# The scan state's decay product on VectorE, the high part of rotated q and k on GpSimd for two heads, and the RWKV output ordered behind a scan step

## The chip, the cores and the metric

The kernel runs on one core of one Trainium2 chip. The metric is the device time of one execution in microseconds (us). Before the change three runs gave 1136.71, 1142.31 and 1142.92 us, a median of 1142.31 us. The five engines have the profile's names here: PE is TensorE, DVE is VectorE, ACT is ScalarE, POOL is GpSimd, SP issues most DMAs.

## The reference, cut to what matters

Two layers of a diffusion backbone run over 512 latent tokens and 256 context tokens, 1024 channels, batch 1, all in float32. In each layer one input projection feeds three groups of mixers, and an output projection joins them. The two mixers that the change touches:

```python
def step(S, inp):                       # RWKV, per direction, 4 heads of 64x64 state
    w_t, k_t, v_t, a_t, b_t = inp[-5:]
    sa = jnp.einsum('bhvk,bhk->bhv', S, a_t)
    S = S * w_t[:, :, None, :] + sa[..., None] * b_t[:, :, None, :] + v_t[..., None] * k_t[:, :, None, :]
    y_t = jnp.einsum('bhvk,bhk->bhv', S, inp[0]) if with_output else None
    return S, y_t
# readout: y = y_fwd + y_bwd, normalised per head, times ln_g, plus ln_b and a bonus times v, times silu(z)

# attention: q and k are rotated by position, then two softmaxes per head are subtracted
q_l = apply_axial_rope(qk_heads(q_l), rope)
k_l = apply_axial_rope(qk_heads(k_l), rope)
p = jax.nn.softmax(s, axis=-1)
attn = p[:, :, 0] - lam * p[:, :, 1]
```

The kernel does not run the recurrence token by token. It works in chunks of 64 tokens: inside a chunk everything is matrix products, and only the state is carried from chunk to chunk.

## The kernel before, in words

**Input projection as filler.** Every float32 weight tile (`wraw`) is split into a high part `whi` (a cast on ACT, L265) and a low part `wlo` (a subtract on POOL or DVE, L268), and each product is three matmuls. These matmuls (tiles pcl, pcc, ptl, ptc, by a helper at L137) are handed out in small amounts by `fill(us)` between the steps of the RWKV scan, so PE has work while the other engines carry the state.

**The scan** (`rwkv_scan`, L841). There are 12 chunks in each direction, taken as 3 batches `b` of 4 steps `p`, both directions side by side: 24 steps in two layers. Ahead of a batch stand a first stage (the products `s`, masked on DVE into `R`, with the diagonal blocks `Dg`) and an inverse of small triangular blocks (tiles `Acc`, `invt`, on DVE). One step is this chain, each part waiting for the one before it:

1. PE: `ch<-zu,R`, 16 small matmuls of the state tile `zu` (values and state, one tile per direction).
2. DVE: two copies `gs<-ch` out of PSUM.
3. PE: `yps<-zu,rt` (ordered behind the second gs copy) and `ch<-gs,XT`.
4. ACT and DVE in turn: four copies `zu<-ch` (ACT at L968, DVE in the same loop).
5. PE: `ch<-zu,R` again.
6. DVE: four adds `zu<-pz,ch` make the state for the next step, where `pz` is the old state times the chunk's decay `pc`.

The product `pz` (L947) is four multiplies of 64x128 elements per step on POOL, 88 in all, since the last step of each layer needs none. It needs only the state at the start of the step; its reader is part 6. The step's output is copied from `yps` on ACT (L991) or added on DVE. The tile framework's scheduler turns the program into one fixed order per engine; an engine takes its instructions strictly in that order.

**Rotated q and k** (`attn_proj`, function `qk`, from L1110). Four heads, q and k, two layers: 16 times. ACT copies the projection into `qkr` (L1118), SP moves the partner halves into `qks` by DMA, then POOL multiplies by sin (L1124) and cos (L1125) and adds (L1126); for heads 2 and 3 (`QV`) cos and add are on DVE. ACT casts the sum into its high part (L1127, over `qks`), POOL (DVE for heads 2 and 3) subtracts for the low part (L1128), and two DMAs (L1129, L1130) store both. This runs inside the filler, so it falls among the scan steps.

**RWKV output** (`rwkv_out`, L1000). For each part of the tokens: values `Vs` are loaded, multiplied by the bonus (L1019) and raised by ln_b (L1021) on POOL; DVE takes the mean `mu`, a variance and a Newton inverse root on tiny tiles (`rs_y`, `rs_t`), and scales `Y`. In layer 0 the part for the context tokens is ready after batch 0; the scheduler may place it anywhere behind that.

Of the kernel before, what the change touches and what calls it, by code (L numbers as in the profile page):

```python
# [26 lines left out]
HD = 64  # L27
# [38 lines left out]
QV = (2,3)  # L66
# [40 lines left out]
def build(tc, A):  # L107
    nc = tc.nc
    ctx = ExitStack()
    S, G = nc.scalar, nc.gpsimd  # L110
# [17 lines left out]
    V = Vec()  # L128
# [63 lines left out]
    def small(n, tag, pool=None, bufs=2):  # L192
        return (pool or sm).tile([P, n], F32, tag=tag, bufs=bufs, name=tag)
# [641 lines left out]
    def rwkv_scan(l, st, rw, lat, cx):  # L835
# [5 lines left out]
        zu = {}  # L841
# [32 lines left out]
        for b in range(3):  # L874
# [44 lines left out]
            for p in range(4):  # L919
# [19 lines left out]
                for d in range(2):  # L939
                    gs[d] = rw.tile([P, 2, HD], F32, tag="gs", bufs=2, name="gs")  # L940
                    cp = V.tensor_copy(gs[d], pv[d][:, 0])
                if not end:
                    for d in range(2):
                        pz[d] = rw.tile([P, 2, HD], F32, tag="pz", bufs=2, name="pz")
                        for h in range(2):
                            hr = slice(h * 64, h * 64 + 64)
                            G.tensor_tensor(out=pz[d][hr], in0=zu[d][hr, :, h, :],  # L947
                                            in1=prepd[d][1][hr, :, cc[d][1]].unsqueeze(2).to_broadcast([64, 2, HD]),
                                            op=ALU.mult)
                fill(F["a"] if want_y else F["n"])  # L950
# [45 lines left out]
                zu = nz  # L996
        lin["on"] = lin["dve"] = False

    def rwkv_out(l, st, yr, rw):
        n = NL if l == L - 1 else NT  # L1000
        zr = rw.tile([P, 2, NT], F32, tag="kkn", name="zr")
        nc.sync.dma_start(out=zr[:, :, :n], in_=zrd[l].rearrange("a p t -> p a t")[:, :, :n])
        Y = st["Y"]
        lng = rw.tile([P, 2, 2, HD], F32, tag="lng", name="lng")
        for h in range(2):
            nc.scalar.dma_start(out=lng[h * 64:h * 64 + 64].rearrange("p a b v -> p (a b v)"),
                                in_=A["lngb"][l, h:h + 1, :].to_broadcast([64, 256]))
        for c0, nch in ((0, 8),) if l == L - 1 else ((8, 4), (0, 8)):
            nu = nch * 2
            Yu = Y[:, c0:c0 + nch].rearrange("p c a v -> p (c a) v")  # L1010
            bon = st["bon"][:, 2 * c0:2 * c0 + nu]
            Vs = rw.tile([P, 8, 2, HD], F32, tag="wk", bufs=WK, name="Vs")
            for h in range(2):
                for hp in range(2):
                    o = hp * P + h * 64
                    nc.sync.dma_start(out=Vs[h * 64:h * 64 + 64, 0:nch, hp, :],
                                      in_=vd[l][c0 * 64:(c0 + nch) * 64, o:o + 64].rearrange("(c t) v -> t c v", t=64))
            Vu = Vs[:, :nch].rearrange("p c a v -> p (c a) v")
            G.tensor_tensor(out=Vu, in0=Vu, in1=bon.unsqueeze(2).to_broadcast([P, nu, HD]), op=ALU.mult)  # L1019
            for hp in range(2):  # L1020
                G.tensor_tensor(out=Vs[:, :nch, hp], in0=Vs[:, :nch, hp],  # L1021
                                in1=lng[:, 1, hp].unsqueeze(1).to_broadcast([P, nch, HD]), op=ALU.add)
            mu = small(24, "mu")
            V.tensor_reduce(out=mu[:, :nu], in_=Yu, axis=AX.X, op=ALU.add)
            V.tensor_scalar_mul(mu[:, :nu], mu[:, :nu], -1.0 / HD)
            V.tensor_tensor(out=Yu, in0=Yu, in1=mu[:, :nu].unsqueeze(2).to_broadcast([P, nu, HD]), op=ALU.add)
            sq = rw.tile([P, 24, HD], F32, tag="wk", bufs=WK, name="gnsq")
            S.activation(sq[:, :nu], Yu, AF.Square)
            var = small(24, "var")
            V.tensor_reduce(out=var[:, :nu], in_=sq[:, :nu], axis=AX.X, op=ALU.add)  # L1030
            V.tensor_scalar(out=var[:, :nu], in0=var[:, :nu], scalar1=1.0 / HD, scalar2=GN_EPS,
                            op0=ALU.mult, op1=ALU.add)
            rs = small(24, "gnrs")
            rsqrt(var[:, :nu], nu, rs[:, :nu])
            V.tensor_tensor(out=Yu, in0=Yu, in1=rs[:, :nu].unsqueeze(2).to_broadcast([P, nu, HD]), op=ALU.mult)
            for hp in range(2):
                yh = Y[:, c0:c0 + nch, hp]
                V.tensor_tensor(out=yh, in0=yh, in1=lng[:, 0, hp].unsqueeze(1).to_broadcast([P, nch, HD]), op=ALU.mult)
                V.tensor_tensor(out=yh, in0=yh, in1=Vs[:, :nch, hp], op=ALU.add)
                fill(F["o"] if hp == 0 else F["o2"])  # L1040
                lin["next"] = MG & 64
                pb = psalt("yT")
                for c in range(nch):
                    for h in range(2):
# [60 lines left out]
    def attn_proj(l, lat, cx):  # L1105
# [8 lines left out]
        def qk(h, fk=()):  # L1114
            for i in range(2):
                t, sw = fst("qkr"), fst("qks")
                yield from proj_ch(l, lat, cx if i else cxx,
                                   lambda o, c, nn: S.mul(t[:, c:c + nn], o, 1.0 if i else 0.125), fk=fk)  # L1118
                nn = NT if i else n
                for j in range(2):  # L1120
                    for x in range(2):
                        a, b = j * 64 + x * 32, j * 64 + 32 - x * 32
                        pin((S if SW else nc.sync).dma_start(out=sw[a:a + 32, :NL], in_=t[b:b + 32, :NL]), 2)
                G.tensor_tensor(out=sw[:, :NL], in0=sw[:, :NL], in1=sinT, op=ALU.mult)  # L1124
                (V if h in QV else G).tensor_tensor(out=t[:, :NL], in0=t[:, :NL], in1=cosT, op=ALU.mult)  # L1125
# [607 lines left out]
```

## Time and profile before

| | |
|---|---|
| runs | 1136.71, 1142.31, 1142.92 us, median 1142.31 |
| the profiled execution | 1136.55 us, of which its span (first to last instruction) is 1134.8 us |
| busy, PE / DVE / ACT / POOL | 1029.8 / 714.8 / 523.7 / 446.5 us |
| share of the span | 91% / 63% / 46% / 39% |
| chain that ended last | PE 41%, DVE 15%, ACT 7%, POOL 6%, issue 6% |
| POOL, wlo (L268) and pz (L947) | 181.6 and 39.5 us busy |

Busy is time in which an engine executes. PE is at 91%, so what can be won lies in its idle stretches and in stretches with a lowered clock; the chain shows that the other engines set the end for about a third of the span. An engine's idle time is put down to what released it ("idle before <-releaser"). L118 is the helper through which all DVE operations go, L137 and L135 the helpers for matmuls, so tiles tell operations apart. Times in the trace count from the start of the span.

### The profile page before, as it was taken

How to read it: one execution, taken by the hardware profiler on the slowest of the kernel's cores; microseconds unless marked ns; L12 is line 12 of the kernel's file. 1: busy time of each engine (PE TensorE's matmuls, PEld its weight loads, DVE VectorE, ACT ScalarE, POOL GpSimd, SP SyncE). 2: the span in 40 equal slices, each digit the busy share in tenths (PEclk: the TensorE clock that was granted, in tenths of full speed). 3: DMA queues.
4: the chain of work that ended last, by engine and by line, in shares of the span. 5: the costliest groups of instructions: out<-in, count | busy, mean ns of one | idle time of the engine just before them, and what ended most of it. 6: DMA issues, size and time to landing. Idle time of an engine off the chain costs nothing.

```text
span 1134.8 us, 25347 instructions
## 1 busy us (share of the span) xinstructions
PE 1029.8 (91%) x9850; PEld 844.0 (74%) x9850; DVE 714.8 (63%) x1736; ACT 523.7 (46%) x1330; POOL 446.5 (39%) x452
## 2 busy tenths in 40 slices
PE   4899989999699998989899899998988999888897
PEld 1577968777588867878787786876767897777775
DVE  3530558788467262489847857776985824579944
ACT  3432553453363223478724564654353532248731
POOL 0311534434736522432222345255475454431322
PEclk9999999999999999989999999999998999999999
DMA  9574322212334466654052452232223345546143
GB/s 354 178 242 134 86 79 57 58 35 71 133 85 130 131 192 194 201 172 103 15 190 85 139 180 86 70 96 71 78 79 103 99 127 160 165 149 183 48 158 111
DMA packets 92088, 142.55 MB, mean 126 GB/s; under 512 B 28192, under 2 KB 36416, under 8 KB 91968
## 3 DMA queue, kind: packets, MB, share of 16 engines
q1 hardware_dynamic: 88512, 136.14, 39.0%
q10 hardware_dynamic: 3456, 4.80, 1.3%
q8 instruction: 77, 1.26, 0.5%
q14 instruction: 43, 0.35, 0.1%
HBM read 110.99 MB, written 25.71 MB: 120 GB/s over the span
## 4 chain that ended last, share of the span: by engine, by line
PE 41%; DVE 15%; ACT 7%; issue 6%; POOL 6%; DMA 3%; SPq 1%; ACTq 0%; DVEq 0%; POOLq 0%
PE pcl L137 14%; PE op L137 6%; PE ptl L137 3%; PE pcc L137 3%; PE av L137 2%; PE ptc L137 2%; PE sc L137 2%; DVE mx L118 2%; PE ch L135 1%; DMA mraw<-in_mod_w_dram 1%; ACT e L1250 1%; DVE bk L118 1%; DVE rs_t L118 1%; PE yps L135 1%; POOL wlo L268 1%
## 5 line engine op out<-in xcount | busy, mean ns | idle before, releaser
L268 POOL TENSOR_TENSOR wlo<-wraw,whi 128x512 fp32r<-128x512 f32 x134 | 181.6, 1358 | 303.1 <-ACT whi L265 261.6
L137 PE MATMUL pcl<-lat,whi 128*128 128x512 f32 (+1 forms) x928 | 294.6, 394 | 2.6 <-issue 1.6
L137 PEld LDWEIGHTS pcl<-lat,whi 128*128 128x128 f32 x928 | 169.8, 190 | 40.0 <-issue 7.5
L137 PE MATMUL pcl<-lat,wlo 128*128 128x512 f32 (+1 forms) x464 | 184.6, 398 | 2.9 <-POOL wlo L268 2.9
L265 ACT CAST whi<-wraw 128x512 fp32r<-128x512 f32 x144 | 88.8, 619 | 149.6 <-DMA wraw<-in_w_in_dram 38.7
L137 PE MATMUL pcc<-ctx,whi 128*128 128x256 f32 x576 | 111.4, 290 | 2.2 <-DVE ctx L118 1.7
L137 PEld LDWEIGHTS pcl<-lat,wlo 128*128 128x128 f32 x464 | 87.8, 189 | 27.1 <-issue 4.5
L137 PEld LDWEIGHTS pcc<-ctx,whi 128*128 128x128 f32 x576 | 94.0, 195 | 9.2 <-issue 3.2
L137 PE MATMUL pcc<-ctx,wlo 128*128 128x256 f32 x288 | 83.7, 291 | 2.0 <-DVE wlo L118 2.0
L137 PE MATMUL ptl<-whi,lat 128*128 128x256 f32 x384 | 79.2, 293 | 0.0
L1250 ACT ACTIVATE e<-sc,mx 128x768 f32<-128x768 f32 (+1 forms) x80 | 66.3, 831 | 15.9 <-DVE mx L118 10.4
L118 DVE TENSOR_REDUCE mx<-sc 128x1 f32<-128x768 f32 (+1 forms) x72 | 63.9, 921 | 14.7 <-PE sc L137 14.7
L137 PE MATMUL av<-vA,aT 128*128 128x128 f32 x416 | 58.7, 285 | 10.1 <-ACT aT L1285 10.0
L137 PEld LDWEIGHTS av<-vA,aT 128*128 128x128 f32 x416 | 54.2, 194 | 16.0 <-ACT aT L1285 12.9
L137 PEld LDWEIGHTS ptl<-whi,lat 128*128 128x128 f32 x384 | 63.1, 195 | 2.0 <-issue 0.5
L118 DVE TENSOR_TENSOR R<-s,cs 128x384 f32<-128x384 f32 (+1 forms) x96 | 47.0, 530 | 19.6 <-PE s L135 18.9
L137 PEld LDWEIGHTS pcc<-ctx,wlo 128*128 128x128 f32 x288 | 55.9, 194 | 4.6 <-DVE wlo L118 2.2
L137 PE MATMUL sc<-KH,QS 128*128 128x256 f32 (+1 forms) x144 | 52.8, 380 | 4.5 <-ACT e L1250 2.9
L947 POOL TENSOR_TENSOR pz<-zu,pc 64x128 f32<-64x128 f32 x88 | 39.5, 449 | 43.2 <-DVE zu L118 38.5
L137 PE MATMUL ptl<-wlo,lat 128*128 128x256 f32 x192 | 56.1, 292 | 0.0
L137 PE MATMUL sc<-KL,QS 128*128 128x256 f32 (+1 forms) x144 | 46.3, 342 | 0.0
L118 DVE COPY zu<-ch 64x128 f32<-64x128 f32 x48 | 14.1, 294 | 47.8 <-ACT zu L968 41.8
(448 smaller groups left out, 2403.6 us busy)
## 6 DMA issues: line engine op xcount, KB each, us to landing
wraw<-in_w_in_dram SPq DMA_DIRECT2D x144, 256.0 KB, 2.7
mraw<-in_mod_w_dram SPq DMA_DIRECT2D x96, 256.0 KB, 4.5
KH<-qd SPq DMA_DIRECT2D x32, 192.0 KB, 3.8
oraw<-in_w_out_dram SPq DMA_DIRECT2D x20, 256.0 KB, 3.6
qd<-qks SPq DMA_DIRECT2D x12, 384.0 KB, 2.3
qd<-qkr SPq DMA_DIRECT2D x12, 384.0 KB, 2.5
qks<-qkr SPq DMA_DIRECT2D x64, 64.0 KB, 2.1
zu<-vd SPq DMA_DIRECT2D x96, 32.0 KB, 2.2
```

The costliest lines, as they stand in the source:

```text
L118: i = f(*a, **k)
L135: tc.keep_in_program_order(nc.tensor.matmul(*a, **k))
L137: i = nc.tensor.matmul(*a, **k)
L265: S.copy(hi, raw)
L268: eng.tensor_tensor(out=lo, in0=raw, in1=hi.bitcast(F32), op=ALU.subtract)
L947: G.tensor_tensor(out=pz[d][hr], in0=zu[d][hr, :, h, :], in1=prepd[d][1][hr, :, cc[d][1]].unsqueeze(2).to_broadcast([64, 2, HD]), op=ALU.mult)
L1250: ac(S.activation(ej[:, c], pb[:, c], AF.Exp, bias=mx[:, i:i + 1], accum_out=den[:, u["h"] * 6 + tt, j:j + 1]))
```

## The change

Three edits. The product `pz` is issued on DVE in place of POOL, 88 operations of 64x128 elements. The cast to the high part of rotated q and k is issued on POOL in place of ACT for heads 0 and 1, 8 of 16 casts (6 of 128x768 elements, 2 of 128x512). In the RWKV output, the bonus multiply on POOL and the mean on DVE are ordered behind the second `gs` copy of batch 2's first step; this is an order for the scheduler, not a semaphore.

```diff
--- before.py
+++ after.py
@@ -939,12 +939,14 @@
                 for d in range(2):
                     gs[d] = rw.tile([P, 2, HD], F32, tag="gs", bufs=2, name="gs")
                     cp = V.tensor_copy(gs[d], pv[d][:, 0])
+                if b == 2 and p == 0:
+                    st["step"] = cp.ins.name
                 if not end:
                     for d in range(2):
                         pz[d] = rw.tile([P, 2, HD], F32, tag="pz", bufs=2, name="pz")
                         for h in range(2):
                             hr = slice(h * 64, h * 64 + 64)
-                            G.tensor_tensor(out=pz[d][hr], in0=zu[d][hr, :, h, :],
+                            V.tensor_tensor(out=pz[d][hr], in0=zu[d][hr, :, h, :],
                                             in1=prepd[d][1][hr, :, cc[d][1]].unsqueeze(2).to_broadcast([64, 2, HD]),
                                             op=ALU.mult)
                 fill(F["a"] if want_y else F["n"])
@@ -1001,6 +1003,11 @@
         zr = rw.tile([P, 2, NT], F32, tag="kkn", name="zr")
         nc.sync.dma_start(out=zr[:, :, :n], in_=zrd[l].rearrange("a p t -> p a t")[:, :, :n])
         Y = st["Y"]
+
+        def behind(i):
+            tc.add_manual_dep(i.ins, st["step"], mybir.DependencyInfo(
+                mybir.DependencyClass.NoSync, mybir.DependencyReason.DATA), reason="order")
+
         lng = rw.tile([P, 2, 2, HD], F32, tag="lng", name="lng")
         for h in range(2):
             nc.scalar.dma_start(out=lng[h * 64:h * 64 + 64].rearrange("p a b v -> p (a b v)"),
@@ -1016,12 +1023,14 @@
                     nc.sync.dma_start(out=Vs[h * 64:h * 64 + 64, 0:nch, hp, :],
                                       in_=vd[l][c0 * 64:(c0 + nch) * 64, o:o + 64].rearrange("(c t) v -> t c v", t=64))
             Vu = Vs[:, :nch].rearrange("p c a v -> p (c a) v")
-            G.tensor_tensor(out=Vu, in0=Vu, in1=bon.unsqueeze(2).to_broadcast([P, nu, HD]), op=ALU.mult)
+            i = G.tensor_tensor(out=Vu, in0=Vu, in1=bon.unsqueeze(2).to_broadcast([P, nu, HD]), op=ALU.mult)
             for hp in range(2):
                 G.tensor_tensor(out=Vs[:, :nch, hp], in0=Vs[:, :nch, hp],
                                 in1=lng[:, 1, hp].unsqueeze(1).to_broadcast([P, nch, HD]), op=ALU.add)
+            behind(i)
             mu = small(24, "mu")
-            V.tensor_reduce(out=mu[:, :nu], in_=Yu, axis=AX.X, op=ALU.add)
+            i = V.tensor_reduce(out=mu[:, :nu], in_=Yu, axis=AX.X, op=ALU.add)
+            behind(i)
             V.tensor_scalar_mul(mu[:, :nu], mu[:, :nu], -1.0 / HD)
             V.tensor_tensor(out=Yu, in0=Yu, in1=mu[:, :nu].unsqueeze(2).to_broadcast([P, nu, HD]), op=ALU.add)
             sq = rw.tile([P, 24, HD], F32, tag="wk", bufs=WK, name="gnsq")
@@ -1124,7 +1133,7 @@
                 G.tensor_tensor(out=sw[:, :NL], in0=sw[:, :NL], in1=sinT, op=ALU.mult)
                 (V if h in QV else G).tensor_tensor(out=t[:, :NL], in0=t[:, :NL], in1=cosT, op=ALU.mult)
                 (V if h in QV else G).tensor_tensor(out=t[:, :NL], in0=t[:, :NL], in1=sw[:, :NL], op=ALU.add)
-                S.copy(sw[:, :nn].bitcast(F32R), t[:, :nn])
+                (S.copy if h in QV else G.tensor_copy)(sw[:, :nn].bitcast(F32R), t[:, :nn])
                 (V if h in QV else G).tensor_tensor(out=t[:, :nn].bitcast(F32R), in0=t[:, :nn], in1=sw[:, :nn], op=ALU.subtract)
                 pin((S if QQ else nc.sync).dma_start(out=qd[l][i, 0, h, :, :nn], in_=sw[:, :nn]), 1)
                 pin(nc.sync.dma_start(out=qd[l][i, 1, h, :, :nn], in_=t[:, :nn]), 1)
```

The scheduler makes a new order from this, on all engines. Three places follow; line numbers behind L947 differ by 2 to 9 between the two.

ScalarE, layer 0, entry to batch 1's scan, before (`XT` is the last copy of the inverse, `zu` and `Y` belong to the step) and then now:

```order
L832 COPY XT_1101<-mg 32x8x32
L1118 ACTIVATE qkr<-pcc 128x256
L832 COPY XT_1102<-mg 32x8x32
L1127 CAST qks<-qkr 128x768
L265 CAST whi<-wraw 128x512
L968 COPY zu<-ch 64x2x64 x2
L991 COPY Y<-yps 128x128 x2
L968 COPY zu<-ch 64x2x64 x2
```

```order
L832 COPY XT_1101<-mg 32x8x32
L1127 ACTIVATE qkr<-pcc 128x256
L832 COPY XT_1102<-mg 32x8x32
L265 CAST whi<-wraw 128x512
L970 COPY zu<-ch 64x2x64 x2
L993 COPY Y<-yps 128x128 x2
L970 COPY zu<-ch 64x2x64 x2
L265 CAST whi<-wraw 128x512
```

The cast of `qks` that stood ahead of the step's `zu` copies is gone from ScalarE; `whi`, which stood behind it, now stands there alone.

GpSimd at the same place, before and then now (`km` is work of the next batch's preparation):

```order
L696 TENSOR_TENSOR km<-km 128x512
L268 TENSOR_TENSOR wlo<-wraw,whi 128x512
L1124 TENSOR_TENSOR qks<-qks,sinT 128x512
L1125 TENSOR_TENSOR qkr<-qkr,cosT 128x512
L1126 TENSOR_TENSOR qkr<-qkr,qks 128x512
L1128 TENSOR_TENSOR qkr<-qkr,qks 128x768
L268 TENSOR_TENSOR wlo<-wraw,whi 128x512
L947 TENSOR_TENSOR pz<-zu,pc 64x128 x4
```

```order
L696 TENSOR_TENSOR km<-km 128x512
L268 TENSOR_TENSOR wlo<-wraw,whi 128x512
L1133 TENSOR_TENSOR qks<-qks,sinT 128x512
L1134 TENSOR_TENSOR qkr<-qkr,cosT 128x512
L1135 TENSOR_TENSOR qkr<-qkr,qks 128x512
L1136 CAST qks<-qkr 128x768
L1137 TENSOR_TENSOR qkr<-qkr,qks 128x768
L268 TENSOR_TENSOR wlo<-wraw,whi 128x512 x3
```

The cast stands between the add and the subtract of the rotation, and the four `pz` of the step behind them are gone.

VectorE, layer 0, batch 0, the second to fourth step, before and then now:

```order
L118 COPY gs<-ch 128x128 x2
L118 COPY zu<-ch 64x2x64 x2
L118 TENSOR_TENSOR zu<-pz,ch 64x2x64 x4
L118 TENSOR_TENSOR R<-s,cs 128x2x192 x2
L118 COPY gs<-ch 128x128 x2
L118 COPY zu<-ch 64x2x64 x2
L118 TENSOR_TENSOR R<-s,cs 128x2x192 x2
L118 TENSOR_TENSOR zu<-pz,ch 64x2x64 x4
L118 TENSOR_TENSOR Y<-Y,yps 128x128 x2
L118 TENSOR_TENSOR R<-s,cs 128x2x192 x2
```

```order
L118 TENSOR_TENSOR pz<-zu,pc 64x128 x4
L118 COPY zu<-ch 64x2x64 x2
L118 TENSOR_TENSOR zu<-pz,ch 64x2x64 x4
L118 TENSOR_TENSOR pz<-zu,pc 64x128 x4
L118 TENSOR_TENSOR R<-s,cs 128x2x192 x2
L118 COPY gs<-ch 128x128 x2
L118 COPY zu<-ch 64x2x64 x2
L118 TENSOR_TENSOR R<-s,cs 128x2x192 x2
L118 TENSOR_TENSOR zu<-pz,ch 64x2x64 x4
L118 TENSOR_TENSOR Y<-Y,yps 128x128 x2
L118 TENSOR_TENSOR pz<-zu,pc 64x128 x4
L118 TENSOR_TENSOR R<-s,cs 128x2x192
```

In the second step the four `pz` stand between the `gs` and the `zu` copies; in the third and fourth they stand right behind the adds of the step before, ahead of the `gs` copies.

VectorE, layer 0, batch 2's first step, before and then now (`mu`, `var`, `rs` belong to the RWKV output of the context tokens):

```order
L118 COPY gs<-ch 128x128 x2
L118 COPY zu<-ch 64x2x64 x2
L118 TENSOR_TENSOR zu<-pz,ch 64x2x64 x4
L118 TENSOR_TENSOR Y<-Y,yps 128x128 x2
L118 COPY gs<-ch 128x128 x2
```

```order
L118 COPY gs<-ch 128x128 x2
L118 TENSOR_REDUCE mu<-Y 128x8
L118 TENSOR_SCALAR mu<-mu 128x8
L118 TENSOR_TENSOR Y<-Y,mu 128x512
L118 COPY zu<-ch 64x2x64
L118 TENSOR_REDUCE var<-gnsq 128x8
L118 COPY zu<-ch 64x2x64
L118 TENSOR_SCALAR var<-var 128x8
L118 TENSOR_SCALAR rs_i<-var 128x8
L118 TENSOR_SCALAR rs_y<-rs_i 128x8
L118 TENSOR_TENSOR rs_t<-rs_y 128x8
L118 SCALAR_TENSOR_TENSOR rs_t<-rs_t,var 128x8
```

Ten operations of the output now stand inside the step, ahead of its state adds; the rest of that chain stands inside the second step. Before, it stood in batch 1's first stage and in batch 2's inverse.

## Rows read from the trace of the kernel before

**Rows 1.** Page, part 1: engine, busy us, share of the span, instructions
```profile
PE 1029.8 (91%) x9850; PEld 844.0 (74%) x9850; DVE 714.8 (63%) x1736; ACT 523.7 (46%) x1330; POOL 446.5 (39%) x452
```

**Rows 2.** Waits by engine: waiter, what it waited for, us, times, longest
```profile
PE ch L137 <- DVE zu L118: 9.4, 9, 5.5
ACT qks L1127 <- POOL qkr L1126: 34.0, 7, 7.5
```

**Rows 3.** Timeline, layer 0, batch 1's first step: start, us, idle before
```profile
305.22 1.26 POOL L1126 TENSOR_TENSOR qkr<-qkr,qks 128x512 f32<-128x512 f32 x1
306.52 0.83 ACT L1127 CAST qks<-qkr 128x768 fp32r<-128x768 f32 x1 [6.71 <-POOL qkr L1126]
309.15 0.37 PE L137 MATMUL ch<-zu,R 128*64 128x64 f32 x1 [5.55 <-DVE zu L118]
```

**Rows 4.** Timeline, layer 1, batch 1's second step
```profile
863.80 0.37 PE L137 MATMUL yps<-zu,rt 64*64 64x64 f32 x1 [4.15 <-ACT Y L991]
```

**Rows 5.** Windows: stretch, length, busy us of PE, PEld, DVE, ACT, POOL, PEclk, DMA
```profile
309.15:313.31 4.16, 4.16 (x50) 3.82 (x52) 2.79 (x6) 0.54 (x2) 3.41 (x6) 0.50 0.66 217
863.80:869.68 5.88, 5.88 (x64) 5.54 (x66) 0.59 (x2) 1.16 (x4) 3.77 (x4) 0.50 0.42 153
214.00:382.00 168.00, 153.65 (x2243) 131.62 (x2242) 108.78 (x271) 71.56 (x206) 89.01 (x92) 0.97 0.31 92
```

**Rows 6.** Tile pz: operation, duration in ns min/median/max
```profile
L947 POOL TENSOR_TENSOR pz<-zu,pc x88: 395/401/944, 123.7 to 948.7; 64x128 f32<-64x128 f32 x88
L118 DVE TENSOR_TENSOR zu<-pz,ch x88: 269/286/293, 219.5 to 953.5; 64x128 f32<-64x128 f32 x88
```

**Rows 7.** Timeline, layer 0, last batch's first step, VectorE, then PE
```profile
385.19 0.49 DVE L118 COPY gs<-ch 128x128 f32<-128x128 f32 x2 [2.06 <-PE ch L135]
387.22 0.29 DVE L118 COPY zu<-ch 64x128 f32<-64x128 f32 x1 [1.54 <-ACT zu L968]
387.85 0.30 DVE L118 COPY zu<-ch 64x128 f32<-64x128 f32 x1 [0.33 <-ACT zu L968]
389.15 1.20 DVE L118 TENSOR_TENSOR zu<-pz,ch 64x128 f32<-64x128 f32 x4 [1.00 <-PE ch L135]
391.36 0.49 DVE L118 COPY gs<-ch 128x128 f32<-128x128 f32 x2 [0.49 <-PE ch L135]
386.25 0.63 PE L135 MATMUL ch<-gs,XT 64*64 64x64 f32 x16
```

**Rows 8.** Timeline, layer 0's inverse, VectorE and GpSimd side by side
```profile
257.80 1.20 DVE L118 TENSOR_TENSOR invt<-Acc 128x72 f32<-128x72 f32 x1
259.11 0.23 DVE L118 TENSOR_TENSOR Acc<-Acc,invt 128x72 f32<-128x72 f32 x1
257.63 1.29 POOL L268 TENSOR_TENSOR wlo<-wraw,whi 128x512 fp32r<-128x512 f32 x1 [0.17 <-ACT whi L265]
```

**Rows 9.** GpSimd groups of the whole run, by line: busy us, mean ns
```profile
L765 POOL COPY Acc<-cs 128x16 f32<-128x16 f32 x12 | 2.2, 222 | 12.8 <-DVE Acc L118 12.8
L864 POOL COPY MS<-I 128x256 f32<-128x256 f32 x2 | 0.8, 400 | 6.7 <-DVE I L118 6.7
L1128 POOL TENSOR_TENSOR qkr<-qkr,qks 128x768 fp32r<-128x768 f32 (+1 forms) x8 | 14.0, 1749 | 4.0 <-ACT qks L1127 4.0
```

**Rows 10.** Timeline, layer 0, VectorE: RWKV output pieces and one Newton step
```profile
247.56 0.68 DVE L118 TENSOR_REDUCE mu<-Y 128x8 f32<-128x512 f32 x1
348.82 0.16 DVE L118 TENSOR_TENSOR rs_t<-rs_y 128x8 f32<-128x8 f32 x1
352.35 0.42 DVE L118 TENSOR_TENSOR Y<-Y,lng 128x256 f32<-128x256 f32 x1
```

**Rows 11.** Timeline, start of layer 0's attention, ScalarE and PE
```profile
498.37 0.83 ACT L1127 CAST qks<-qkr 128x768 fp32r<-128x768 f32 x1 [0.84 <-DVE qkr L118]
486.38 0.50 PE L137 MATMUL sc<-KH,QS 128*128 128x512 f32 x1 [1.66 <-ACT qkr L1118]
501.52 1.65 PE L137 MATMUL av<-vA,aT 128*128 128x128 f32 x6 [2.61 <-ACT aT L1285]
```

## The prediction

> **What bounds the kernel now.** I read the page's busy times first: PE is busy 1029.8 us, 91% of the span [rows 1], so VectorE's and GpSimd's loads matter only where PE stands still for them. Then the waits by engine. PE's list has one entry in the scan with a single stall of 5.5 us, `ch` behind VectorE's `zu` copy; ScalarE's list shows the same places from the other side: the `qks` cast waited 34.0 us in 7 times for GpSimd's add, 7.5 us at the longest [rows 2]. The timeline shows how these belong together. In layer 0 GpSimd's add ran from 305.22 to 306.48, the cast behind it on ScalarE had waited 6.71 us, and PE stood 5.55 us until 309.15 [rows 3]: ScalarE takes its instructions in order, so the `zu` copies behind the cast waited for a rotation with which the scan has nothing to do. In layer 1 the instruction caught behind the cast is a `Y` copy, whose PSUM tile PE wants back for `yps`: 4.15 us [rows 4]. Last, the windows: right behind both stalls PE is busy without a gap at a granted clock of 0.50, which is 1.2 GHz of 2.4, for 4.16 and 5.88 us [rows 5]. The stall is paid once while it lasts and again behind it.
>
> **Edit 2, the cast on GpSimd: the gain.** For heads 0 and 1 the cast leaves ScalarE, and with it the wait; both stalls are behind such casts. Idle time that can go: 5.55 + 4.15 = 9.7 us. With no stall ahead of them the two half-clock stretches should run at full clock; at half clock half of the time is lost: 4.16/2 + 5.88/2 = 5.0 us. Together 14.7 us. What is late next is the ordinary chain of a step; and GpSimd's own chain gets longer by the cast. A GpSimd cast of 128x768 is not in the trace. Two one-input copies are: 0.222 us for 16 elements and 0.400 for 256 [rows 9], a slope of 0.74 ns an element, so about 0.78 us for 768; the two-input subtract of 1.75 is the upper end and 0.40 the lower. The subtract and the next `wlo` come later by 0.78 less the handover to ScalarE and back that goes. I leave 0.6 us for both places as what remains of the stalls. GpSimd's 8 casts are some 6 us, against 39.5 that it loses by edit 1. The other five of the seven waits set no PE stall, so nothing is counted for them.
>
> **Edit 1, `pz` on VectorE.** 88 operations. Their nearest row on VectorE is the add of the same shape, 0.286 us, four of them in 1.20 us [rows 6, 7]; one of its inputs is in PSUM. With both inputs in SBUF the nearest rows are `invt` and `Acc`: 0.23 us with GpSimd quiet, but 1.20 us for the one that began at 257.80 while GpSimd's `wlo` ran from 257.63 to 258.92; the next, when GpSimd was done, took 0.23 [rows 8]. So a `pz` that comes under a GpSimd instruction ends when that one ends. A group of four costs 1.24 us (0.31 apart) when GpSimd is quiet; under back-to-back GpSimd work about two pass for each 1.28 us, so 2.6. The ends are thus 88 x 0.27 = 24 us and 22 x 2.6 = 57 us of VectorE time; I take 1.24 a group, since GpSimd is busy 89.0 of 168 us in layer 0's scan [rows 5]; less its own 32 `pz` of 0.40 us that is a share of 0.45.
>
> The Trainium skill, page "SBUF — State Buffer", section "Who interferes with whom", has this as a rule: a VectorE instruction with two SBUF inputs contends with a GpSimd instruction that reads SBUF, and the second to issue blocks fully until the first is done. It speaks against this edit, and the rows just named agree with it. The first rival below is this rule applied to every group.
>
> What of these 22 groups lies on the path, by the new order on VectorE: 6 stand in preparation, first stage or behind the inverse, off the path. 4 stand between `gs` and `zu` copies, where VectorE now idles 1.54 us [rows 7]: 1.24 fits, cost nothing. 7 stand whole ahead of `gs`, 5 in two parts around it. Ahead of `gs` VectorE idles 0.49 us, and `ch<-gs` begins at 386.25, 0.57 us behind the copies' end at 385.68 [rows 7]; a whole group costs 1.24 - 0.49 - 0.57 = 0.2 us, 1.4 for the seven; a split one with three ahead (0.93) nothing. If that cover were gone it would be 1.24 for each of 16 groups, 20 us.
>
> Meeting GpSimd costs more. At the two steps behind the casts GpSimd runs the rotation without a pause, so the group takes 2.6 in place of 1.24; some is covered, I take 1.0 each: 2.0. For the other 14 groups on the path the chance that GpSimd is at work is 0.45 and the rest of its instruction 0.64 us (half of 1.28): 0.29 each, 4.0 in all, half of it under the idle just named: 2.0. Below nothing these costs cannot go by their own doing: in the steps shown the add waits for PE (1.00 us), not for `pz` [rows 7].
>
> **Edit 3, the output behind a scan step.** In layer 0 some of the context's chain now stands in batch 2's first two steps. First step, ahead of the `zu` copies: `mu` 0.68, a tiny one 0.16, `Y` less `mu` about 0.68, 1.52 in all under 1.54 of idle; between the copies `var`, priced as `mu`, 0.68 over 0.33: 0.35 late; ahead of the adds five tiny ones, 0.8 under 1.00. Second step: a `pz`, seven tiny ones (0.16 each) and one 0.68 make 2.1 against 1.54, 0.55 late; between the copies three of 0.42 with 0.33 idle, 0.9 late [rows 7, 10]. Sum 1.8 us; the ends are nothing, if PE's filler covers it, and 3.6, if each of them is doubled by GpSimd. What it leaves, batch 1's first stage and the inverse of batch 2, gets shorter on VectorE, but PE has filler there: no gain. In layer 1 the order moves the bonus multiply on GpSimd into batch 2's steps; its meeting with `pz` is within the 2.0 above.
>
> **The sum.** -14.7 + 0.6 + 1.4 + 2.0 + 2.0 + 1.8 = -6.9 us. The profiled execution took 1136.55 (its span 1134.8 and 1.75 around it), so a like execution takes 1129.6. It was the low end of the runs shown, whose median is 5.8 above it; I expect the new runs to scatter alike: 1135.4, called 1135.
>
> **Rivals.**
> A. GpSimd blocks most groups. For it: rows 8 show the block, and GpSimd's `wlo` is ready in many steps. Against it: with `pz` gone GpSimd stands still for half of the time. If every group took 2.6 us: seven whole ones 2.6 - 1.06 = 1.5 each, five split ones 0.9, four behind `gs` 1.1, together 19.4 us, with 1.8 + 0.6 a cost of 21.8 against 14.7: 1142.3 + 7.1 = 1149, slower. It decides from about two thirds of the 16 groups blocked.
> B. The stall only moves: rotation, cast and subtract now are one string on GpSimd, and `wlo`, `pz` or the filler's matmuls come late where the `zu` copies did. For it: the string is three instructions of some 1.26 us, the cast, and 1.75 more. Against it: the copies on ScalarE no longer stand behind it, and PE's filler there uses weights split earlier. With half of the 14.7 left: 1142.3 - 7.35 + 7.2 = 1142.
> C. The start of layer 0's attention improves too. The scheduler there puts the rotation's add of the later heads ahead of a softmax maximum and moves ScalarE's cast, which began at 498.37 ahead of an `aT` copy; PE stood 1.66 and 2.61 us there [rows 11]. Were both gone, 4.3 more: 1131; with edit 1 at no cost besides (5.4 us), 1126. Against it: heads 2 and 3 keep the cast on ScalarE, and nothing in the edit aims there.
> D. The change does not do what it says at one of the two places: the `zu` copies still stand behind something that waits. The new order has a `whi` cast there, which waits for its buffer; then one stall stays, some 7 us: 1142, as B.
>
> **Chances.** My forecast 0.53 (own range 1129 to 1141), A 0.14, B with D 0.21, C 0.12. A difference under 0.5%, 5.7 us, can hardly be told from no change here. Faster by more, below 1136.6: 0.36 of my case's 0.53, all of C, 0.03 of B: 0.51. Slower by more, above 1148: 0.10 of A, 0.03 of the others: 0.13. The rest, 0.36, is the same. The range runs from C's lower end, 1126, less a microsecond for the scatter of runs, to A's 1149.
>
> **What would show it.** In the new profile: no PE stall of 4 us at the two steps, and no half-clock stretch behind them; ScalarE's `zu` copies right behind PE's `ch`. `pz` on VectorE with a median near 0.27 us and a tail to 1.3; if the median itself is near 1, A holds. PE stalls of 0.2 to 1 us ahead of `ch<-gs` or `ch<-zu` in several steps are my cost. I am wrong if the stalls stay under another releaser (B, D), if PE's idle time in the steps sums to more than 15 us (A), or if the difference stands in the attention (C).

## The result, and the profile after

The changed kernel's 22 runs gave a median of 1147.7 us (1141.6 to 1154.0), the 22 of the kernel before 1139.99 us (1132.2 to 1149.7). The ratio is 1.0064, 95% interval 1.0041 to 1.0087 (the two medians alone give 1.0068): the change makes the kernel slower by 0.6%, where 0.6% faster was forecast. The time lies in the range given; the direction was wrong.

The profiled execution took 1145.58 us (span 1143.8, 9.0 longer than before). The page of the changed kernel, the line that answers to [rows 1]:

```profile
PE 1029.7 (90%) x9850; PEld 842.8 (74%) x9850; DVE 750.3 (66%) x1824; ACT 519.2 (45%) x1322; POOL 411.5 (36%) x372
```

PE's busy time is the same to 0.1 us, so the whole difference is time in which PE stood. PE's waits, which answer to [rows 2] (waiter, what it waited for, us in total, times, longest); the first line is the kernel before, the others the changed one:

```profile
PE s L137 <- DVE R L118: 5.4, 6, 1.7
PE ch L137 <- DVE zu L118: 12.5, 14, 3.5
PE s L137 <- DVE R L118: 9.5, 9, 2.0
PE ch L135 <- DVE gs L118: 2.3, 4, 1.0
```

Before, `s` waited 5.4 us in 6 times for `R`, now 9.5 in 9: this is the first stage, where PE makes `s` and VectorE must mask it into `R` before PE can make the next. And `ch` behind the `zu` copies still has a stall of 3.5 us. For the windows both traces are cut at the first `gs` copy of each of the 24 steps (some cuts, in the experiments below too, lie up to 0.4 us ahead of it, which moves a sum of four stretches by 0.5 us at most). The four stretches between two batches (fourth step, first stage, inverse), before and then after (stretch, length, busy us of PE, PEld, DVE, ACT, POOL, granted clock, DMA):

```profile
235.93:300.30 64.37, 56.87 (x774) 47.79 (x774) 51.78 (x115) 29.00 (x76) 31.90 (x29) 1.00 0.24 73
327.94:385.19 57.25, 56.49 (x857) 50.87 (x856) 33.29 (x91) 26.02 (x70) 32.00 (x29) 0.97 0.41 119
794.88:853.05 58.17, 53.04 (x680) 41.79 (x680) 51.42 (x100) 25.58 (x60) 36.08 (x35) 1.00 0.26 74
881.02:935.90 54.88, 53.34 (x846) 48.53 (x845) 29.23 (x71) 23.21 (x61) 29.51 (x27) 1.00 0.38 113
```

```profile
234.93:300.96 66.03, 56.36 (x769) 47.09 (x767) 52.88 (x116) 28.81 (x77) 30.55 (x26) 1.00 0.23 69
326.37:384.98 58.61, 56.08 (x853) 50.36 (x852) 26.27 (x77) 24.04 (x67) 25.68 (x22) 0.97 0.32 96
796.44:858.34 61.90, 54.62 (x689) 42.50 (x689) 56.08 (x108) 27.28 (x68) 34.23 (x27) 1.00 0.25 71
885.22:942.21 56.99, 54.55 (x854) 49.59 (x854) 27.87 (x77) 24.29 (x67) 27.21 (x23) 1.00 0.38 112
```

Length less PE's busy time is its idle time: 7.5 + 0.8 + 5.1 + 1.5 = 14.9 us before, 9.7 + 2.5 + 7.3 + 2.4 = 21.9 after. In these stretches PE's waits of `s` for `R` went from 2.1 us in 3 times to 6.2 in 7, and those of `ch` for `zu` from 2.0 in 3 to 4.4 in 4; one of 0.9 us of `ch` for `gs` is new, and the others hardly moved. The third stretch shows `R` late: VectorE's last two `R` began 8.8 us behind the cut before, and 13.5 us behind it now (first line before, second now):

```profile
803.68 1.01 DVE L118 TENSOR_TENSOR R<-s,cs 128x384 f32<-128x384 f32 x2
809.91 1.02 DVE L118 TENSOR_TENSOR R<-s,cs 128x384 f32<-128x384 f32 x2
```

The same working for the whole span:

| PE idle, us | before | after |
|---|---|---|
| start to the first step | 23.9 | 23.2 |
| the four stretches between batches | 14.9 | 21.9 |
| layer 0, batch 1, steps 1 to 3 (one old stall) | 5.8 | 3.2 |
| layer 0, batch 2, steps 1 to 3 (the output chain) | 0.0 | 1.9 |
| layer 1, batch 1, steps 1 to 3 (the other old stall) | 5.4 | 5.1 |
| the other steps | 3.3 | 5.2 |
| between the scans (attention, output, next layer's start) | 27.6 | 29.9 |
| behind the last scan | 24.2 | 23.7 |

Layer 0's stall went, layer 1's didn't, and 7.0 us came between the batches. Layer 0's stall left a small one, at the next step. VectorE, ScalarE, GpSimd and PE there (start, us, operation, idle before), to be read against [rows 3]:

```profile
309.06 0.49 DVE L118 COPY gs<-ch 128x128 f32<-128x128 f32 x2
309.58 3.18 DVE L118 TENSOR_TENSOR pz<-zu,pc 64x128 f32<-64x128 f32 x4
312.79 0.29 DVE L118 COPY zu<-ch 64x128 f32<-64x128 f32 x1
310.93 0.26 ACT L970 COPY zu<-ch 64x128 f32<-64x128 f32 x1 [5.19 <-DVE pz L118]
308.56 2.14 POOL L1137 TENSOR_TENSOR qkr<-qkr,qks 128x768 fp32r<-128x768 f32 x1
310.66 1.33 POOL L268 TENSOR_TENSOR wlo<-wraw,whi 128x512 fp32r<-128x512 f32 x1
313.76 0.27 PE L137 MATMUL ch<-zu,R 128*64 128x64 f32 x1 [1.86 <-DVE zu L118]
```

Four `pz` took 3.18 us in place of 1.2, two of them under GpSimd's instructions, and ScalarE's first `zu` copy waited for the first of them. Layer 1, batch 1's second step, the place of [rows 4]:

```profile
865.65 0.49 DVE L118 COPY gs<-ch 128x128 f32<-128x128 f32 x2
866.17 4.86 DVE L118 TENSOR_TENSOR pz<-zu,pc 64x128 f32<-64x128 f32 x4
871.07 0.29 DVE L118 COPY zu<-ch 64x128 f32<-64x128 f32 x1
866.99 0.26 ACT L970 COPY zu<-ch 64x128 f32<-64x128 f32 x1 [1.30 <-DVE pz L118]
865.03 1.71 POOL L1134 TENSOR_TENSOR qkr<-qkr,cosT 128x512 f32<-128x512 f32 x1
866.83 1.29 POOL L1135 TENSOR_TENSOR qkr<-qkr,qks 128x512 f32<-128x512 f32 x1
868.18 0.82 POOL L1136 CAST qks<-qkr 128x768 fp32r<-128x768 f32 x1
869.09 1.80 POOL L1137 TENSOR_TENSOR qkr<-qkr,qks 128x768 fp32r<-128x768 f32 x1
872.03 0.37 PE L137 MATMUL ch<-zu,R 128*64 128x64 f32 x1 [3.53 <-DVE zu L118]
```

Here the four took 4.86 us. They ran beside cos, add, cast and subtract of the rotation, which GpSimd took without a pause: one `pz` for each GpSimd instruction. VectorE's `zu` copy stands behind all four in VectorE's own order and came at 871.07; PE stood 3.53 us. The stall of 4.15 us has changed its releaser from ScalarE's `Y` copy to VectorE's `zu`. All `pz` of the changed kernel, which answer to [rows 6] (tile view: ns min/median/max; groups: busy us, mean ns):

```profile
L118 DVE TENSOR_TENSOR pz<-zu,pc x88: 273/289/1874, 127.2 to 957.2; 64x128 f32<-64x128 f32 x88
```

```profile
L118 DVE TENSOR_TENSOR pz<-zu,pc 64x128 f32<-64x128 f32 x88 | 36.6, 416 | 3.3 <-POOL zu L925 1.6
```

The median, 0.289 us, is near the forecast 0.27. 36.6 us busy less 88 times 0.289 leaves 11.2 us, put down here to being blocked: 15 of the 88 took more than 0.33 us.

### The profile page after: what moved, and what is told of

Same layout as the page of the kernel before. It is cut to its first block, busy times and chain, and to the rows that moved or that the text cites. A ratio compares the mean times of both kernels' runs of the same rounds, so it can differ in the third digit from the quotient of the medians.

```text
span 1143.8 us, 25292 instructions
## 1 busy us (share of the span) xinstructions
PE 1029.7 (90%) x9850; PEld 842.8 (74%) x9850; DVE 750.3 (66%) x1824; ACT 519.2 (45%) x1322; POOL 411.5 (36%) x372
## 4 chain that ended last, share of the span: by engine, by line
PE 30%; DVE 20%; ACT 6%; issue 5%; POOL 2%; DMA 2%; SPq 0%; DVEq 0%; ACTq 0%; POOLq 0%
PE pcl L137 8%; PE op L137 7%; DVE mx L118 3%; PE pcc L137 3%; PE ptl L137 2%; DVE e L118 2%; PE av L137 1%; DMA mraw<-in_mod_w_dram 1%; PE ptc L137 1%; DVE pz L118 1%; PE sc L137 1%; DVE bk L118 1%; DVE qkr L118 1%; DVE zu L118 1%; PE ch L135 1%
## 5 line engine op out<-in xcount | busy, mean ns | idle before, releaser
L268 POOL TENSOR_TENSOR wlo<-wraw,whi 128x512 fp32r<-128x512 f32 x134 | 179.2, 1341 | 375.9 <-ACT whi L265 340.7
L137 PE MATMUL pcl<-lat,whi 128*128 128x512 f32 (+1 forms) x928 | 298.4, 396 | 1.7 <-POOL lat L353 1.3
L137 PE MATMUL pcc<-ctx,whi 128*128 128x256 f32 x576 | 108.5, 286 | 2.0 <-DVE ctx L118 1.7
L118 DVE SCALAR_TENSOR_TENSOR e<-e,cf,e 128x512 f32<-128x512 f32 (+1 forms) x72 | 46.8, 683 | 0.5
L145 PE MATMUL aTp<-ident,e 128*128 128x128 f32 x208 | 37.4, 289 | 9.2 <-DVE zT L118 4.7
```

Of the source, the lines that this page charges most:

```text
L118: i = f(*a, **k)
L137: i = nc.tensor.matmul(*a, **k)
L145: i = nc.tensor.transpose(*a, **k)
L268: eng.tensor_tensor(out=lo, in0=raw, in1=hi.bitcast(F32), op=ALU.subtract)
```

## The experiments

Each kernel (6 to 12 runs) was compared with the kernel before on the same chip; the idle times are those of one profiled execution each. Edit 1 is `pz` on VectorE, edit 2 the cast on GpSimd, edit 3 the order of the RWKV output. A group is the four `pz` of one step. "Between" is PE's idle time in the four stretches between batches; "layer 0" and "layer 1" are batch 1's first three steps there, idle time plus the time that the half clock took (length times 1 less PEclk), so that a stall counts with what follows it.

| run | edits | ratio (95%) | between | layer 0 | layer 1 |
|---|---|---|---|---|---|
| before | | 1 | 14.9 | 5.8+3.5 | 5.4+3.5 |
| the change | 1, 2, 3 | 1.0064 (1.0041 to 1.0087) | 21.9 | 3.2+1.7 | 5.1+3.4 |
| e1_pz_only | 1 | 1.0123 (1.0079 to 1.0168) | 23.6 | 5.0+3.4 | 6.1+3.4 |
| e2_cast_only | 2 | 0.9994 (0.9960 to 1.0028) | 19.5 | 2.1+0 | 6.1+1.7 |
| e3_behind_only | 3 | 1.0007 (0.9968 to 1.0045) | 13.6 | 5.8+3.5 | 5.2+1.7 |
| e4_cast_behind | 2, 3 | 0.9955 (0.9924 to 0.9986) | 14.6 | 2.1+0 | 6.1+3.4 |
| e5_pz_cast | 1, 2 | 1.0060 (1.0029 to 1.0090) | 21.2 | 3.4+1.7 | 5.2+1.7 |
| e6_p0_pool | change, first steps' `pz` on GpSimd | 1.0072 (1.0039 to 1.0104) | 19.9 | 3.2+1.8 | 5.0+3.4 |
| e9_pz_act | change, all `pz` on ScalarE | 0.9980 (0.9953 to 1.0007) | 21.4 | 1.6+0 | 3.1+1.8 |
| e10_step_act | 2, 3, one step's `pz` on ScalarE | 0.9903 (0.9867 to 0.9939) | 14.2 | 1.3+0 | 2.6+0 |
| e11_p0_dve | 2, 3, first steps' `pz` on VectorE | 0.9927 (0.9887 to 0.9967) | 16.4 | 2.2+0 | 6.0+3.4 |
| e12_p23_dve | 2, 3, third and fourth steps' `pz` on VectorE | 1.0009 (0.9978 to 1.0040) | 18.1 | 2.7+0 | 5.9+3.5 |
| e13_after_step_act | change, one step's `pz` on ScalarE | 1.0000 (0.9969 to 1.0031) | 20.7 | 2.3+0 | 3.9+0 |
| e14_step_act_free | as e10 without 3 | 0.9954 (0.9915 to 0.9994) | 14.8 | 1.6+0 | 2.7+0 |

**The edits one by one.** These runs are the change with the other edits undone. The code fences show changed lines alone; `...` stands for what is left out between them.

e1_pz_only, against the change:
```diff
-(S.copy if h in QV else G.tensor_copy)(sw[:, :nn].bitcast(F32R), t[:, :nn])
+S.copy(sw[:, :nn].bitcast(F32R), t[:, :nn])
...
-            behind(i)
...
-            behind(i)
```


> Edit 1 alone: the product pz on VectorE, cast back on ScalarE, output chain unordered. The changed kernel shows 7.0 us more PE idle time between the batches (first stage and inverse), where VectorE is busy without a pause. Theory S (first stage): VectorE is the bound there and every pz and every R that it pushes back is paid, so edit 1 alone costs the whole of it, and the two old stalls (5.55 and 4.15 us) stay on top: ratio 1.008 to 1.013, PE idle between the batches up by 5 to 7 us. Theory B (GpSimd's blocking is what costs): with the rotation broken up by ScalarE's cast the long blocked groups shorten, ratio 1.002 to 1.006, and idle between batches up by less than 3.

Measured 1.0123, inside theory S's range and beyond theory B's; between the batches 8.7 us came, more than S's 5 to 7. Both old stalls stayed. In layer 1 the four `pz`, now on VectorE, were done at 877.54, and PE still stood as long as before, for the `Y` copy behind ScalarE's cast:

```profile
877.86 0.37 PE L137 MATMUL yps<-zu,rt 64*64 64x64 f32 x1 [4.15 <-ACT Y L993]
```

e2_cast_only, against the change:
```diff
-V.tensor_tensor(out=pz[d][hr], in0=zu[d][hr, :, h, :],
+G.tensor_tensor(out=pz[d][hr], in0=zu[d][hr, :, h, :],
...
-            behind(i)
...
-            behind(i)
```


> Edit 2 alone: the cast of heads 0 and 1 on GpSimd, pz stays on GpSimd. If the recorded gain of the cast is real (9.7 us of stall and about 5 of half clock), and pz behind the rotation on GpSimd isn't late: both stalls gone, ratio 0.987 to 0.993. Rival: pz stands behind the rotation, cast and low weights on GpSimd's queue, and the state adds wait for it in the stall's place: ratio 0.997 to 1.002, with a PE gap of 3 us or more released by VectorE's adds or copies at one of the two steps.

Measured 0.9994: the rival. Its trace gives two reasons. In layer 1 ScalarE, GpSimd and PE show:

```profile
865.26 0.26 ACT L970 COPY zu<-ch 64x128 f32<-64x128 f32 x1 [3.88 <-POOL pz L949]
867.97 0.26 ACT L970 COPY zu<-ch 64x128 f32<-64x128 f32 x1 [2.45 <-POOL pz L949]
864.04 0.82 POOL L1134 CAST qks<-qkr 128x768 fp32r<-128x768 f32 x1
864.83 0.40 POOL L949 TENSOR_TENSOR pz<-zu,pc 64x128 f32<-64x128 f32 x1
865.19 1.79 POOL L1135 TENSOR_TENSOR qkr<-qkr,qks 128x768 fp32r<-128x768 f32 x1
867.06 1.35 POOL L949 TENSOR_TENSOR pz<-zu,pc 64x128 f32<-64x128 f32 x3
868.79 0.27 PE L137 MATMUL ch<-zu,R 128*64 128x64 f32 x1 [4.43 <-DVE zu L118]
```

The `zu` copy, no longer behind a cast, waits for `pz`. The kernel says why: it copies into `zu[d][0:64, :, 0, :]`, the very half of the tile that `pz` reads as the old state. The copy may not overwrite it before. The kernel before has it as well, which the prediction did not take in:

```profile
865.87 0.26 ACT L968 COPY zu<-ch 64x128 f32<-64x128 f32 x1 [1.43 <-POOL qkr L1128]
862.68 0.87 POOL L947 TENSOR_TENSOR pz<-zu,pc 64x128 f32<-64x128 f32 x2
863.73 1.81 POOL L1128 TENSOR_TENSOR qkr<-qkr,qks 128x768 fp32r<-128x768 f32 x1 [0.18 <-ACT qks L1127]
865.49 0.87 POOL L947 TENSOR_TENSOR pz<-zu,pc 64x128 f32<-64x128 f32 x2
```

Two of the step's `pz` stood behind the subtract and began at 865.49; the `zu` copy began at 865.87, when the first of them (0.40 us long) was done. The cast held the `Y` copies; `pz` held the `zu` copies behind them. Each by itself keeps layer 1's stall: with `pz` off GpSimd and the cast left it was 4.15 us (e1), with the cast moved and `pz` left 4.43 (here), and with both moved (e10 below) it is gone. The second reason is a new stall in layer 0, in batch 2's inverse (GpSimd, VectorE, PE):

```profile
358.81 1.90 POOL L1026 TENSOR_TENSOR Vs<-Vs,bon 128x1024 f32<-128x1024 f32 x1
360.67 1.27 POOL L268 TENSOR_TENSOR wlo<-wraw,whi 128x512 fp32r<-128x512 f32 x1
361.91 1.25 POOL L1028 TENSOR_TENSOR Vs<-Vs,lng 128x512 f32<-128x512 f32 x1
363.13 1.25 POOL L268 TENSOR_TENSOR wlo<-wraw,whi 128x512 fp32r<-128x512 f32 x1
358.97 1.83 DVE L118 TENSOR_TENSOR Acc<-Acc,invt 128x72 f32<-128x72 f32 x1
360.83 1.18 DVE L118 TENSOR_TENSOR invt<-Acc 128x52 f32<-128x52 f32 x1
362.05 1.19 DVE L118 TENSOR_TENSOR Acc<-Acc,invt 128x52 f32<-128x52 f32 x1
363.27 1.16 DVE L118 TENSOR_TENSOR invt<-Acc 128x28 f32<-128x28 f32 x1
366.89 0.20 PE L137 MATMUL mg<-T,Bm 32*32 32x16 f32 x1 [5.48 <-DVE T L118]
```

GpSimd ran from 351.38 to 365.60 without a pause, and each of VectorE's small products, some 0.2 us by itself, lasted as long as one GpSimd instruction.

e3_behind_only keeps the output's `behind` alone:
```diff
-V.tensor_tensor(out=pz[d][hr], in0=zu[d][hr, :, h, :],
+G.tensor_tensor(out=pz[d][hr], in0=zu[d][hr, :, h, :],
...
-(S.copy if h in QV else G.tensor_copy)(sw[:, :nn].bitcast(F32R), t[:, :nn])
+S.copy(sw[:, :nn].bitcast(F32R), t[:, :nn])
```


> Edit 3 alone: output chain of the context tokens ordered behind batch 2's first scan step. In the changed kernel the two steps that carry it show 1.9 us more PE idle. Theory: that is its cost here too, ratio 1.001 to 1.003. Rival: it takes VectorE work out of batch 1's first stage, where PE waits for VectorE, and gains there what it costs in the steps: ratio 0.998 to 1.000.

The steps that carry the chain cost 0.9 us of idle, half of what they cost in the change, and PE idles 1.3 us less in the stretches between batches, as its rival had it; the ratio of 1.0007 decides for neither.

e5_pz_cast, against the change:
```diff
-            behind(i)
...
-            behind(i)
```


> Edits 1 and 2 without 3. VectorE and PE have the same order as in the run with edit 1 alone, so the difference between the two is the cast's place and nothing else: theory S gives 5 to 8 us less than edit 1 alone (layer 0's stall gone, layer 1's kept by the blocked pz), ratio 1.003 to 1.006 to before. If the cast is worth its full 14.7 us with pz on VectorE, ratio 0.998 to 1.000.

1.0060 against 1.0123 of edit 1 alone: the cast is worth 0.6%, some 7 us, about half of the 14.7 forecast, as theory S had it (the ratio at the edge of its range). In these two traces layer 0's steps give 3.3 us of it (8.4 to 5.1), layer 1's 2.6 (9.5 to 6.9), most of that as half clock.

e4_cast_behind undoes edit 1 alone:
```diff
-V.tensor_tensor(out=pz[d][hr], in0=zu[d][hr, :, h, :],
+G.tensor_tensor(out=pz[d][hr], in0=zu[d][hr, :, h, :],
```


> Edits 2 and 3 without 1 (pz stays on GpSimd). With edit 2 alone layer 0's stall went (5.55 us), but a new one of 5.48 came in batch 2's inverse, where GpSimd's rotation and values run without a pause beside VectorE's inverse and the output chain. Theory: edit 3 takes that chain out of the inverse, so the new stall shrinks to under 1.5 us; layer 1's 4.4 us stays, since there the zu copies wait for pz behind the rotation on GpSimd. Ratio 0.992 to 0.997. Rival: the inverse stays blocked by GpSimd and edit 3 adds its own steps' idle: ratio 0.999 to 1.003.

As the theory said: 0.9955, the inverse's stall gone, layer 1's kept. Edits 2 and 3 gain 0.45%, 5 us; against this run edit 1 costs 1.1%, 12 us. The inverse's stall of e2 is gone with edit 3's order, though the two ratios' intervals overlap.

**Where edit 1's cost lies.** e6_p0_pool:
```diff
-V.tensor_tensor(out=pz[d][hr], in0=zu[d][hr, :, h, :],
+(V if p else G).tensor_tensor(out=pz[d][hr], in0=zu[d][hr, :, h, :],
```


> The changed kernel with the pz of each batch's first step (24 of 88, those that stand in the first stage) back on GpSimd. Theory S: the first stage is bound by VectorE, and these 24 cost what they last there: PE idle between the batches falls by 3 to 5 us of the 7.0 added, ratio to before 1.002 to 1.004. Rival: what costs between the batches is the new order of R and the copies, not these products: idle falls by less than 1.5 us, ratio 1.005 to 1.008.

Idle fell by 2.1 us, between the two ranges, and the ratio stayed, as the rival had it: theory S, that the products in the first stage itself are the cost, fell. A new theory, S2, takes VectorE's time in the scan as a whole for what is short. Its test is the complement, e11_p0_dve (against e4):
```diff
-G.tensor_tensor(out=pz[d][hr], in0=zu[d][hr, :, h, :],
+(G if p else V).tensor_tensor(out=pz[d][hr], in0=zu[d][hr, :, h, :],
```


> Edits 2 and 3, with pz on VectorE for each batch's first step alone (24 of 88, mostly in the first stage), on GpSimd for the others. The complement of the run that put these 24 back on GpSimd: there PE's idle time between the batches fell by only 2.1 us of 7.3. Theory S2 (VectorE's time in the scan as a whole is what is short; the products of the later steps push R and the diagonal blocks into the first stage): these 24 alone add 1 to 3 us between the batches, ratio 0.997 to 1.000 against 0.9955 without them. Rival: the first stage's own products are the cost: 5 us or more, ratio 1.000 to 1.003.

and e12_p23_dve (against e4):
```diff
-G.tensor_tensor(out=pz[d][hr], in0=zu[d][hr, :, h, :],
+(G if p < 2 else V).tensor_tensor(out=pz[d][hr], in0=zu[d][hr, :, h, :],
```


> Edits 2 and 3, with pz on VectorE for the third and fourth step of each batch (the steps in whose idle time VectorE masks R for the next batch), on GpSimd for the first and second. Theory S2: these push R out of the steps, so PE waits for R in the first stage: PE idle between the batches 3 to 5 us above the 14.6 of the run with edits 2 and 3, ratio 0.999 to 1.002. Rival: the products fit into the steps' idle time and cost under 1.5 us between the batches, ratio 0.995 to 0.997.

Above e4's 14.6 us between the batches, 24 products cost 1.8, the 40 of the third and fourth steps 3.5, 64 (e6) 5.2, all 88 7.3: the idle time grows with the number of products, as S2 has it. But e1 and e5, with the same order on VectorE and PE, differ by 2.4 us here, so the 1.8 of e11 is not clear of the scatter. The times divide edit 1's 1.1% otherwise. e11 missed its range (0.997 to 1.000): 0.9927 shows no cost beside e4's 0.9955, and e6 shows none beside the change, so no run shows that the first steps' 24 products cost time. The 40 of the third and fourth steps cost some 0.5% (1.0009 beside 0.9955; e12's interval lies wholly above e11's), as S2 had it. The rest, some 0.6% (e6's 1.0072 beside 1.0009; their intervals just touch), is the second steps', and the next run tells where in them. Not separated is plain load from blocking: in the change four products in these stretches were blocked (1.31, 0.48, 0.82 and 1.02 us), some 2.5 us above their 0.289.

**The blocked groups.** e13_after_step_act adds to the change:
```diff
+if b == 1 and p == 1:
+    for hp in range(2):
+        S.activation(pz[d][hr, hp], zu[d][hr, hp, h, :], AF.Identity,
+                     scale=prepd[d][1][hr, hp, cc[d][1]:cc[d][1] + 1])
+    continue
```


> The changed kernel with pz on ScalarE in batch 1's second step of each layer alone, the two groups that GpSimd's instructions blocked on VectorE (3.18 and 4.86 us for four). Theory: the blocked groups hold the zu copies; without them layer 1's stall of 3.53 us falls under 1.5, layer 0's 1.86 under 1, with their half-clock stretches, and the rest of the cost (between the batches) stays: ratio 0.999 to 1.003. Rival: what blocks is the state of the step and not the products' engine: both gaps stay, 1.005 to 1.008.

1.0000: both stalls and their half clock went (layer 0 4.9 to 2.3, layer 1 8.5 to 3.9; the longest wait left there is 1.65 us, for `gs` at the next step), the rest stayed. Two of 22 groups cost about as much as the whole change lost to the kernel before.

e10_step_act adds the same to e4:
```diff
+if b == 1 and p == 1:
...
+    continue
```


> Edits 2 and 3, pz on GpSimd except in batch 1's second step of each layer, where it is on ScalarE: the one group that stands behind a rotation on GpSimd. Theory W: the zu copies overwrite the state that pz reads, so they wait for pz, and layer 1's stall (4.4 us with the cast on GpSimd, 4.15 before) is set by pz and not by the cast: it falls under 1 us and its half-clock stretch goes, ratio 0.4 to 0.6% below the run with edits 2 and 3, 0.987 to 0.992 to before. Rival: something else on GpSimd or ScalarE holds that step, and a gap of 3 us or more stays there.

0.9903, the fastest of all, faster than both kernels (its interval overlaps e4's). ScalarE, VectorE and PE at layer 1's step:

```profile
856.73 0.26 ACT L975 COPY zu<-ch 64x128 f32<-64x128 f32 x1 [1.30 <-PE ch L135]
857.35 0.26 ACT L975 COPY zu<-ch 64x128 f32<-64x128 f32 x1 [0.36 <-DVE zu L118]
857.02 0.29 DVE L118 COPY zu<-ch 64x128 f32<-64x128 f32 x1 [1.12 <-ACT zu L975]
858.20 0.27 PE L137 MATMUL ch<-zu,R 128*64 128x64 f32 x1
```

The `zu` copy waits for PE's `ch` again, and `ch<-zu,R` starts with no idle time: theory W.

e9_pz_act, against the change:
```diff
-V.tensor_tensor(out=pz[d][hr], in0=zu[d][hr, :, h, :],
...
+for hp in range(2):
+    S.activation(pz[d][hr, hp], zu[d][hr, hp, h, :], AF.Identity,
+                 scale=prepd[d][1][hr, hp, cc[d][1]:cc[d][1] + 1])
```


> The changed kernel with every pz on ScalarE, as eight scaled copies of 64x64 in place of four products of 64x128. ScalarE is not in the exchange of ports between VectorE and GpSimd. Theory: layer 1's stall (3.53 us, four pz of 0.72 to 1.87 us each) and layer 0's 1.86 go, and the first stage gets VectorE back: ratio 0.990 to 0.998. Rival: eight copies of some 0.2 us stand in ScalarE's order ahead of the zu copies and of the diagonal blocks, and PE waits for those instead: ratio 1.000 to 1.008.

0.9980, at the edge of the theory's range: the stalls shrank, but between the batches PE idled 21.4 us. There ScalarE's `zu` copies came late behind the scaled copies and the diagonal blocks: `ch` waited 8.0 us in 4 times for `zu` (2.0 in 3 before), as the rival had it. The profiled execution was the longest of the twelve (1145.69 us, median 1137.95), so its idle times may be more than the usual. A scaled copy of 64x64 took 0.34 us at the median, where 0.2 was expected.

e14_step_act_free, against e10:
```diff
-            behind(i)
...
-            behind(i)
```


> The best run so far (edits 2 and 3, pz on GpSimd, on ScalarE in batch 1's second step) without edit 3. Theory: edit 3 is what keeps batch 2's inverse clear: without it the stall of some 5.5 us in front of the inverse's products comes back, 0.9 us of idle in the two steps go, ratio 0.993 to 0.997. Rival: the inverse's stall came from the place of GpSimd's rotation and is gone with the new order: ratio 0.987 to 0.991.

Its trace has no stall in the inverse, so the rival was right about that. Its ratio lies where the theory put it, for no reason that the trace shows: the profiled execution was the shortest of the twelve (1126.7 us, median 1137.32). The intervals of e10 and e14 overlap. Whether edit 3 earns anything in this version stays open.

## Why the prediction was wrong

1. **"6 stand in preparation, first stage or behind the inverse, off the path", and 0.2 us for a whole group.** This step failed: edit 1 was priced at 1.4 + 2.0 + 2.0 = 5.4 us and cost 1.1%, some 12 (the change beside e4). I priced each group against the idle time of its own step. That idle time already had users: in the third and fourth steps VectorE masks `R` for the next batch. With `pz` in it, `R` slides into the first stage, where PE waits for it. I had 1.4 us for groups on the path and 0 off it; the runs show 7.3 us of idle time between the batches for the 88, and some 0.5% of time for the 40 of the third and fourth steps. The runs' times show that these 40 cost and that the first steps' own 24 do not (e6, e11, e12); how much of the cost is blocking stays open.
2. **"What is late next is the ordinary chain of a step", and 0.6 us for what remains of the stalls.** This step failed by as much: edits 2 and 3 were priced at -14.7 + 0.6 + 1.8 = -12.3 us and gave some -5 without edit 1 (e4). The description ahead of the prediction names the adds as the only readers of `pz`, and "in the steps shown the add waits for PE (1.00 us), not for `pz`" is true; but the `zu` copies wait for it as well, since they overwrite what it reads. So layer 1's stall had two causes in a row, and taking away the cast left the second. Of 14.7 us of gain, layer 0 gave 9.3 - 4.9 = 4.4 in the change (e13: 7.0), layer 1 8.8 - 8.5 = 0.3. Rival B, the stall only moves, was right there. Either miss by itself would have brought the forecast of -6.9 us to about nothing; both together turned its sign.
3. **"under back-to-back GpSimd work about two pass for each 1.28 us".** It was one for each instruction: 4.86 us for four. Forecast was a cost of 1.0 us for each of the two groups; in the change against e13 they cost 2.6 and 4.6 with the half clock.
4. **Rival A** had the right sign, and its 1149 lies close to 1147.7, but by luck: it wanted two thirds of the groups blocked. 15 of 88 products were, and the worst stood where the chain was tight. The page "SBUF — State Buffer" of the Trainium skill, section "Who interferes with whom", says that the second to issue blocks until the first is done; the rows at 866.17 agree, with one VectorE instruction for each of GpSimd's.
5. **Right:** the price of a free `pz` (0.27 forecast, median 0.289), of the cast (0.78 forecast, 0.82 at 868.18), that layer 0's old stall stood on the cast, and edit 3's 1.8 us in its steps (1.9 in the change, 0.9 without edit 1; its effect on the time is not told from none). That edit 3 would gain nothing in batch 2's inverse was not: with `pz` on GpSimd a stall of 5.48 us there (e2) is gone once its order is added (e4).

## What to carry to other kernels

Before an operation moves to an engine with idle time, list who uses that idle time already and what those are late for; and list not only who reads its result, but who overwrites its inputs. A stall with one named releaser may have a second one close behind: look at what else in that queue the waiting instruction needs, then test it by moving that one instruction. Moving two groups of products to a third engine went with 0.5 to 0.6% less time (e10 beside e4, e13 beside the change); moving all 88 to VectorE cost 1.1%.

## What the runs showed of the hardware that was not expected

A blocked VectorE instruction of 0.29 us took 0.72, 1.34, 0.85 and 1.87 us beside GpSimd instructions of 1.71, 1.29, 0.82 and 1.80: beside a cast with one input as well as beside instructions with two. And one and the same order of work can differ by more than the whole effect of the change: from the start to the first scan step the change and e13 have the same instructions in the same order on PE, VectorE, ScalarE and GpSimd, yet that part took 213.84 us at a granted clock of 0.98 in the one profiled execution and 220.68 us at 0.95 in the other. That is why one profiled execution's time says little about half a per cent.
